# Two weight issues on ScalarE's queue, the first queries between the memory's keys and values, and one more rest on VectorE

## The chip, the cores and the metric

The kernel runs on one core of a Trainium2 chip. The core has TensorE (PE; its weight loads are shown as PEld), VectorE (DVE), ScalarE (ACT), GpSimd (POOL) and SyncE (SP), each with an instruction queue of its own that runs in order, and 16 DMA engines. The metric is device time of one launch, in microseconds, as the median of three runs.

## The reference

One inference step of a one-layer encoder, in float32: 512 prompt tokens and 32 sample tokens with d = 1024.

```
z  = rmsnorm(x, g) @ w_in                     # 3880 columns: qa ka va ga qb kb vb gb qm gm qi ki wi
mk, mv = split(rmsnorm(mem, g_mem) @ w_mem_kv, 2)
oa = band attention(qa, ka, va, bias table)   # 6 heads, own chunk of 64 and 8 before it
ob = attention over the k keys with the highest index score (qi, ki, wi)   # k = 128 prompt, 256 sample
om = attention(qm, mk, mv)                    # 4 heads, 256 memory tokens
x  = x + concat(oa*silu(ga), ob*silu(gb), om*silu(gm)) @ w_out
y  = rmsnorm(x, g_final)
```

The sample's 32 tokens do the same against caches of earlier keys and values. The new keys and values are outputs too.

## The kernel before

Every dense product of the prompt runs as three products of rounded parts: an operand x is split into a high part h (rounded to the format in which TensorE runs fastest) and a rest l = x - h, and x w is h wh + l wh + h wl. In the names, `xTh` and `xTl` are the parts of the scaled, transposed input, `wh` and `wl` those of a weight tile, `mTh` and `mTl` those of the memory. ACT makes the high parts, DVE the rests of x, and a rest of a weight (`tsub`, line 672) is made by GpSimd unless the tile's number stands in `WV` (line 36), in which case by DVE. The first four weight tiles, numbers 0 to 3, are the indexer's (296 columns: 8 index heads, the index key, the head weights), and DVE makes their rests in any case (line 665). Numbers 4 to 7 are ka's, four tiles of 256 rows and 384 columns.

The start (lines 803 to 1085) loads x and the index weights in K tiles of 128 rows, eight of them, two to an `x_load`. For each K tile SP issues a DMA of x (`xr`, 128x544) and one of the weights (`raw`, 128x296); for the first one also the norm's weights `g_mix`. Then SP issues two small tables, ka's weights, the rows of x for the norms, and so on. TensorE begins with matmuls of a tile of ones, which fill its time until the first data is there, and then runs `index_group`: for each K tile three pieces (h wh, h wl, l wh) of three matmuls of 128x296, one for each of the prompt's tiles 1 to 3. More fills with ones go between the pieces. Behind it come packed matmuls of the sample (`raw,xF`), of the first tile's keys (`xr,gw`), and the dense matmuls of ka. The accumulators of the index stage are given back when DVE has rotated them (`rot`, `rt`) and ACT has copied the head weights (`wI`); that of `xr,gw` when ACT has copied it (`k`).

After that the projections follow in the order of `EARLY` and `LATE` (lines 45 and 46), and beside them, as tasks, the indexer's scores, the top-k choice, the three attentions and the sample's share. The sample's index scores are `KSs,QSs`: KSs holds 1024 cached index keys and the new ones, split by ACT and DVE. The sample's threshold is found by a search of sixteen steps in a row, each with two passes on ACT and a one-column matmul (`bf_ok`).

No engine chooses at run time what to do next. When the program is built, a planner (class `Line`) keeps a clock for every engine, with costs for each instruction and rates for transfers (`rate`, line 232). Each task waits until a point of this clock, and so the clock sets the order in which instructions are written into the queues. `warm` (line 916) writes fills with ones where the planner's clock sees TensorE waiting in the index stage. So a changed cost or table can move instructions anywhere behind it, without changing what is computed. Nearly all instructions pass through one helper and have its line, L405; they are told apart by their tiles.

Of the kernel before, what the change touches and what calls it, by code (L numbers as in the profile page):

```python
# [27 lines left out]
QA, KA, VA, GA, QB, KB, VB, GB, QM, GM, QI = 0, 384, 768, 1152, 1536, 1920, 2304, 2688, 3072, 3328, 3584  # L28
# [4 lines left out]
TOPK_S = 256  # L33


WV = (0, 1, 2, 3)
START = "xxxtwwwwrrrrrwmmrr"
SURE = 1.0
SLACK = 1.1
# [2 lines left out]
WARM = 0.1  # L42
LATER = 0.3

EARLY = ("ka", "va", "mk", "mv", "qa0", "qa1", "ga0", "qa2", "ga1", "ga2", "qm0", "gm0", "qm1", "gm1")
LATE = ("gb0", "kb", "qb", "vb", "gb1", "gb2")


class Op:


    def __init__(self, eng, d, share, deps):
        self.eng, self.d, self.share, self.deps = eng, d, share, deps
        self.start = self.end = 0.0
        self.after = {}
# [5 lines left out]
class Free:  # L61


    eng = None
# [24 lines left out]
        return When(self.of, self.by)  # L89


class Line:

    def __init__(self):
        self.clk = {"PE": 1.35, "DVE": 0.7, "ACT": 0.9, "POOL": 1.2, "SP": 0.7}

        self.queue = {e: deque() for e in self.clk}  # L100
        self.base = dict(self.clk, DMA=0.0, array=(0.0, 0.0, 0.0, True))
        self.base.update({"DVE port": 0.0, "POOL port": 0.0})
        self.last = self.base.copy()
        self.writes, self.reads, self.users = {}, {}, {}
        self.boxes = {}
        self.tables = {"exp": (AF.Exp, AF.Tanh)}
        self.table = None
        self.mode, self.short = None, False
        self.tasks = []
        self.seq = 0  # L110
        self.margin = 0.3
        self.time = 0.0
        self.warm = None

    def cost(self, eng, op, outs, ins, kw):
        if eng == "PE":
            n = outs[0].free_size()
# [38 lines left out]
    @staticmethod  # L156
    def lag(of, to):

        if of is None and to == "PE":
            return 0.3  # L160
        if of == to or of is None:
            return 0.127 if to == "DVE" else 0.09 if to == "POOL" else 0.0
        return 0.95 if of == "SP" else 0.26 if to == "PE" else 0.2 if of == "PE" else 0.06 if of == "POOL" else 0.15

    def box(self, x):

# [55 lines left out]
    @staticmethod  # L222
    def shares(op, outs, ins):

        if outs[0].space == PSUM or any(x.space == PSUM for x in ins):
            return False
        full = [x for x in ins if x.free_size() > 1]
        if op in ("scalar_tensor_tensor", "tensor_tensor"):
            return True
        return op in ("tensor_scalar", "tensor_copy") and len(full) > 0 and outs[0].dtype == F32  # L230

    def rate(self):

        t = self.clk["SP"]
        return 340e3 if t < 1 else 170e3 if t < 2.3 else 330e3 if t < 7 else 380e3

    def op(self, eng, op, outs, ins, kw):
        deps = {}
        outs_, ins_ = ([x for x in xs if x.tensor.name in self.writes] for xs in (outs, ins))
        for x in outs_ + ins_:  # L240
            b = self.box(x)
            for w, o in self.writes[x.tensor.name]:
                if all(p[0] < q[1] and q[0] < p[1] for p, q in zip(w, b)):
                    if o.eng is None:
                        for u in o.users.values():
                            deps.setdefault(u, False)
                    else:
                        deps[o] = True
        for x in outs_:
            b = self.box(x)  # L250
            for (w, _), o in self.reads[x.tensor.name].items():
                if all(p[0] < q[1] and q[0] < p[1] for p, q in zip(w, b)):
                    deps.setdefault(o, False)
        d = (outs[0].size() * 4 / self.rate() if eng == "SP" else
             self.cost(eng, op, outs, ins, kw) * (1.0 if eng == "PE" else SLACK))
        share = eng == "POOL" or eng == "DVE" and self.shares(op, outs, ins)
        new = Op(eng, d, share, [(o, w) for o, w in deps.items()])
        for x in outs_:
            n, b = x.tensor.name, self.box(x)
            self.writes[n] = [e for e in self.writes[n]  # L260
                              if not all(q[0] <= p[0] and p[1] <= q[1] for p, q in zip(e[0], b))] + [(b, new)]
            self.reads[n] = {k: o for k, o in self.reads[n].items()
                             if not all(q[0] <= p[0] and p[1] <= q[1] for p, q in zip(k[0], b))}
        for x in ins_:
            self.reads[x.tensor.name][self.box(x), eng] = new
        for x in outs_ + ins_:
            self.users[x.tensor.name][eng] = new

        now = self.now()
        for q in self.queue.values():  # L270
            while q and q[0].start <= now:
                q.popleft().enter(self.base)
        self.queue[eng].append(new)
        if share and self.queue["POOL" if eng == "DVE" else "DVE"]:
            self.last = self.base.copy()
            self.events()
        else:
            self.begin(new, self.start(new))
# [9 lines left out]
    def begin(self, o, t):  # L288
        last = self.last
        o.start = t  # L290
        if o.eng == "SP":
            o.end = max(t + 1.3, last["DMA"]) + o.d
            o.after = {"SP": t + 0.45, "DMA": o.end}
        else:
            d = o.d
            if o.eng == "PE":
                (self.window, self.busy, self.over, self.slow) = last["array"]
                d = self.array(t, d)
            o.end = t + d
            o.after = {o.eng: o.end}  # L300
            if o.eng == "PE":
                o.after["array"] = (self.window, self.busy, self.over, self.slow)
            if o.share:
                o.after[o.eng + " port"] = o.end
        o.enter(last)
        self.clk[o.eng] = o.end if o.eng != "SP" else t

    def events(self):

# [124 lines left out]
def hybrid_step(ctx: ExitStack, tc: tile.TileContext, a: dict):  # L434
    ctx.enter_context(tc.manual_schedule())
    nc = tc.nc
    line = Line()
    V, G, A, PE, DMA = (Timed(line, n, e) for n, e in (("DVE", nc.vector), ("POOL", nc.gpsimd), ("ACT", nc.scalar),
                                                       ("PE", nc.tensor), ("SP", nc.sync)))

    def pool(stack, name, side):
        return Slots(line, stack.enter_context(tc.tile_pool(name=name, bufs=1, side=side, reuse_waits="tile")))
# [65 lines left out]
    ka = va = ysS = None  # L508

    queried, gates = [None] * 3, [None] * 3  # L510
    mk = cp.tile([P, 2, 256], F32, tag="mk", name="mk")
    mv = cp.tile([P, 2, 256], F32, tag="mv", name="mv")
# [25 lines left out]
    def tsub(eng, out, in0, in1):  # L538
        eng.tensor_tensor(out, in0, in1, op=ALU.subtract)

    def f(t):
        return t.bitcast(F32)
# [34 lines left out]
    w_in, w_out, w_mem = a["w_in"], a["w_out"], a["w_mem_kv"]  # L577
    NATURAL = {"i": (QI, 296), "ka": (KA, 384), "va": (VA, 384), "kb": (KB, 384), "qb": (QB, 384), "vb": (VB, 384)}
    TURNED = {"qa": QA, "ga": GA, "qm": QM, "gm": GM, "gb": GB}
    for nm in ("i",) + EARLY + LATE:  # L580
        if nm in NATURAL:
# [49 lines left out]
    def w_split():  # L631
        at = {}
        for i in range(len(w_list)):
# [37 lines left out]
            yield line.at(wh) - 0.2  # L671
            tsub(V if i in WV else G, wl, raw, f(wh))
            split.append((wh, wl))
# [131 lines left out]
    def x_load():  # L805

        c = len(x_raw)
        yield from ()
        t = (rp.tile([P, 2, N], F32, tag="xr", name="xr", bufs=3) if c < 3 else
             cp.tile([P, 2, N], F32, tag="gate1", name="xr"))  # L810
        if c % 2 == 0:
            firsts.append(cp.tile([P, 2, 2, 296], F32, tag=("q0", "gate0")[c // 2], name="raw"))
        raw = firsts[c // 2][:, c % 2]
        for kk in range(2):
            rows = slice((2 * c + kk) * P, (2 * c + kk + 1) * P)
            if c == kk == 0:
                DMA.dma_start(t[:, kk, :], a["x_t"][rows, :])
                DMA.dma_start(gT[0], a["norm_mix_g"])
            DMA.dma_start(raw[:, kk, :], w_in[rows, QI:QI + 296])
            if c + kk > 0:  # L820
                DMA.dma_start(t[:, kk, :], a["x_t"][rows, :])
        raws.append(raw)
        x_raw.append(t)
# [80 lines left out]

    over = {}
    line.until(lambda g=x_load(): next(g, 1) == 1)
    make_identity(nc, ident)
    G.memset(nhalf, -0.5)
# [38 lines left out]
    for nm in ("cos32", "sin32", "cos64", "sin64"):  # L947
        d = int(nm[3:])
# [968 lines left out]
    line.spawn(out_sample())  # L1917
    projections(EARLY)
    projections(LATE)
# [206 lines left out]
```

## Time and profile before

| | us |
|---|---|
| median of three runs | 353.21 (352.42 to 353.29) |
| the profiled execution | 352.53 |
| its span on the core | 350.8 |
| PE busy (2748 matmuls) | 342.6, 98% of the span |
| PEld busy | 300.2, 86% |
| DVE busy | 277.5, 79% |
| ACT busy | 224.2, 64% |
| POOL busy | 174.3, 50% |

The span is what the rows below divide; some 1.7 us of the execution lie around it. Matmuls are pipelined and their ends are modelled, so PE's busy share says that it had work, not that it ran at its peak. The distance between the starts of two matmuls is the better measure of their cost.

### The profile page before, as it was taken

The page shows a single profiled execution, that of the slowest core. Times are in us where ns is not written, and L with a number is a line of the kernel's source. Part 1 is how long each engine was busy: PE and PEld are TensorE (multiplying, and loading weights), DVE is VectorE, ACT ScalarE, POOL GpSimd, SP SyncE. Part 2 cuts the span into 40 slices and gives each one's busy share as a digit, 9 for nine tenths or more (in the row PEclk, how much of TensorE's full clock was granted, in tenths as well). Part 3 has the DMA queues.
Part 4 walks back from the last instruction along what each step waited for, and adds up shares of the span by engine and source line. Part 5 has one row for each costly group of instructions (what it writes and reads, how often), then busy time and mean ns, then how long its engine had stood idle before and what let it go on. Part 6 is the DMA issues. An engine that isn't in the chain of part 4 may idle for free.

```text
span 350.8 us, 7580 instructions
## 1 busy us (share of the span) xinstructions
PE 342.6 (98%) x2748; PEld 300.2 (86%) x2748; DVE 277.5 (79%) x700; ACT 224.2 (64%) x536; POOL 174.3 (50%) x195
## 2 busy tenths in 40 slices
PE   8999999999999999999999999999999999999992
PEld 8979989989999998898898899899986777676882
DVE  3765768699889999997999945798996899674743
ACT  5759678898564876894757427413795786472542
POOL 3468264475554585255634473744471465215622
PEclk9999999999999999999999999999999999999998
DMA  7999542456538251343231232232372537300033
GB/s 230 323 360 354 134 140 75 143 162 152 151 92 296 66 144 39 78 127 88 76 91 45 93 124 58 60 93 98 95 284 92 180 106 265 114 0 2 0 111 143
DMA packets 39604, 46.31 MB, mean 132 GB/s; under 512 B 5360, under 2 KB 32624, under 8 KB 39568
## 3 DMA queue, kind: packets, MB, share of 16 engines
q1 hardware_dynamic: 39568, 45.85, 42.0%
q8 instruction: 21, 0.34, 0.4%
q14 instruction: 15, 0.12, 0.1%
HBM read 39.67 MB, written 6.16 MB: 131 GB/s over the span
## 4 chain that ended last, share of the span: by engine, by line
PE 95%; DVE 1%; ACT 1%; issue 1%; POOLq 0%; POOL 0%; ACTq 0%; DVEq 0%
PE bank L405 95%; DVE rot L405 1%; DVE xr L405 0%; ACT junkS L405 0%; DVE rt L405 0%; ACT wh L405 0%; ACT sq L405 0%; POOLq L2114 0%; POOL xr L405 0%; ACT bf_ok L405 0%; ACT k L405 0%; POOL ss L405 0%; ACT wI L405 0%; DVE ones L405 0%; ACTq L405 0%
## 5 line engine op out<-in xcount | busy, mean ns | idle before, releaser
L405 POOL TENSOR_TENSOR wl<-raw,wh 128x512 fp32r<-128x512 f32 (+1 forms) x69 | 104.5, 1523 | 79.9 <-ACT wh L405 68.2
L405 ACT ACTIVATE wh<-raw 128x512 fp32r<-128x512 f32 (+2 forms) x77 | 50.7, 662 | 23.4 <-PE bank L405 12.0
L405 PE MATMUL bank<-wh,xTh 128*128 128x384 f32 (+1 forms) x184 | 61.2, 347 | 0.2 <-ACT k L405 0.2
L405 PE MATMUL bank<-wl,xTh 128*128 128x384 f32 (+1 forms) x184 | 58.8, 334 | 0.0
L405 PE MATMUL bank<-wh,xTl 128*128 128x384 f32 (+1 forms) x184 | 58.5, 332 | 0.0
L405 ACT ACTIVATE z<-z,st 128x256 f32<-128x256 f32 (+3 forms) x80 | 42.4, 553 | 18.9 <-DVE st L405 18.7
L405 PE MATMUL bank<-xTh,wh 128*128 128x272 f32 x208 | 46.3, 303 | 0.0
L405 PE MATMUL bank<-xTl,wh 128*128 128x272 f32 x208 | 43.0, 288 | 0.0
L405 PE MATMUL bank<-xTh,wl 128*128 128x272 f32 x208 | 42.9, 288 | 0.0
L405 PEld LDWEIGHTS bank<-wh,xTh 128*128 128x128 f32 x184 | 34.1, 190 | 1.8 <-ACT wI L405 0.6
L405 PEld LDWEIGHTS bank<-xTh,wh 128*128 128x128 f32 x208 | 32.7, 189 | 2.7 <-issue 1.8
L405 PEld LDWEIGHTS bank<-wl,xTh 128*128 128x128 f32 x184 | 34.1, 190 | 0.0
L405 PEld LDWEIGHTS bank<-wh,xTl 128*128 128x128 f32 x184 | 33.9, 189 | 0.1
L405 PEld LDWEIGHTS bank<-xTl,wh 128*128 128x128 f32 x208 | 32.6, 188 | 0.0
L405 PEld LDWEIGHTS bank<-xTh,wl 128*128 128x128 f32 x208 | 32.6, 189 | 0.0
L405 DVE MAX8 m<-ysel 128x8 f32<-128x256 f32 (+2 forms) x48 | 26.5, 552 | 0.1
L405 DVE MATCH_REPLACE8 ysel<-m,ysel 128x256 f32<-128x256 f32 (+2 forms) x48 | 26.0, 542 | 0.0
L405 PE MATMUL bank<-ident,z 128*128 128x128 f32 (+1 forms) x162 | 24.8, 274 | 0.0
L405 ACT ACTIVATE junkS<-ysS,bi 128x1056 int8<-128x1056 f32 x16 | 18.8, 1172 | 6.8 <-DVE bi L405 5.7
L405 PEld LDWEIGHTS bank<-ident,z 128*128 128x128 f32 (+1 forms) x162 | 18.6, 140 | 5.1 <-issue 1.6
L405 ACT COPY z<-bank 128x512 f32<-128x512 f32 (+2 forms) x31 | 15.7, 520 | 10.2 <-PE bank L405 8.5
L405 DVE SCALAR_TENSOR_TENSOR ysel<-r,wI,ysel 128x256 f32<-128x256 f32 (+2 forms) x21 | 19.7, 938 | 2.4 <-ACT r L405 1.8
(299 smaller groups left out, 784.1 us busy)
## 6 DMA issues: line engine op xcount, KB each, us to landing
raw<-in_w_in_dram SPq DMA_DIRECT2D x20, 384.0 KB, 3.7
raw<-in_w_in_dram SPq DMA_DIRECT2D x26, 256.0 KB, 2.9
raw<-in_w_out_dram SPq DMA_DIRECT2D x16, 256.0 KB, 3.6
xr<-in_x_t_dram SPq DMA_DIRECT2D x8, 272.0 KB, 4.4
nat<-in_x_prompt_dram SPq DMA_DIRECT2D x4, 512.0 KB, 7.7
raw<-in_w_mem_kv_dram SPq DMA_DIRECT2D x8, 256.0 KB, 2.7
xr<-in_x_prompt_dram SPq DMA_DIRECT2D x4, 512.0 KB, 3.3
out_dram<-xr SPq DMA_DIRECT2D x4, 512.0 KB, 2.6
```

The lines of the kernel that those rows point to most:

```text
L405: return fn(*args, **kw)
```

## The change

Three things are edited by hand. The index weights of the first two K tiles (the first `x_load`) are issued on ACT's queue (`DMA2`), beside SP's. In `EARLY` the first tile of qa comes between the memory's keys mk and its values mv. And `WV` has a fifth number, 7: the rest of ka's fourth weight tile is made by DVE. The planner learns of the second queue ("ACTQ"), and its rate of transfers becomes 250 GB/s for the first microsecond and 380 GB/s behind it. Everything else that moves is moved by the planner's clock.

```
-WV = (0, 1, 2, 3)
+WV = (0, 1, 2, 3, 7)
-EARLY = ("ka", "va", "mk", "mv", "qa0", "qa1", "ga0", "qa2", "ga1", "ga2", "qm0", "gm0", "qm1", "gm1")
+EARLY = ("ka", "va", "mk", "qa0", "mv", "qa1", "ga0", "qa2", "ga1", "ga2", "qm0", "gm0", "qm1", "gm1")
+QUEUES = "SP", "ACTQ"
...
-        self.clk = {"PE": 1.35, "DVE": 0.7, "ACT": 0.9, "POOL": 1.2, "SP": 0.7}
+        self.clk = {"PE": 1.35, "DVE": 0.7, "ACT": 0.9, "POOL": 1.2, "SP": 0.7, "ACTQ": 0.7}
...
-        return 340e3 if t < 1 else 170e3 if t < 2.3 else 330e3 if t < 7 else 380e3
+        return 250e3 if t < 1 else 380e3
...
-        if o.eng == "SP":
+        if o.eng in QUEUES:
             o.end = max(t + 1.3, last["DMA"]) + o.d
-            o.after = {"SP": t + 0.45, "DMA": o.end}
+            o.after = {o.eng: t + 0.45, "DMA": o.end}
...
+    DMA2 = Timed(line, "ACTQ", nc.scalar)
...
-            DMA.dma_start(raw[:, kk, :], w_in[rows, QI:QI + 296])
+            (DMA2 if c == 0 else DMA).dma_start(raw[:, kk, :], w_in[rows, QI:QI + 296])
```

The helper's line is L408 in the changed kernel. Its first rows on TensorE's queue, in the index stage, read so before (`ones` is the fill, xTh and xTl the parts of x, x10 that ten follow one another):

```order
L405 MATMUL bank<-ones 128x128 x10
L405 MATMUL bank<-wh,xTh_81 128x296 x3
L405 MATMUL bank<-wl,xTh_81 128x296 x3
L405 MATMUL bank<-wh,xTl_83 128x296 x3
L405 MATMUL bank<-ones 128x128 x3
L405 MATMUL bank<-wh,xTh_81 128x296 x3
L405 MATMUL bank<-wl,xTh_81 128x296 x3
L405 MATMUL bank<-wh,xTl_83 128x296 x3
L405 MATMUL bank<-wh,xTh_81 128x296 x3
L405 MATMUL bank<-wl,xTh_81 128x296 x3
L405 MATMUL bank<-ones 128x128 x2
L405 MATMUL bank<-wh,xTl_83 128x296 x3
```

and so now:

```order
L408 MATMUL bank<-ones 128x128 x9
L408 MATMUL bank<-wh,xTh_81 128x296 x3
L408 MATMUL bank<-wl,xTh_81 128x296 x3
L408 MATMUL bank<-wh,xTl_83 128x296 x3
L408 MATMUL bank<-wh,xTh_81 128x296 x3
L408 MATMUL bank<-ones 128x128 x3
L408 MATMUL bank<-wl,xTh_81 128x296 x3
L408 MATMUL bank<-wh,xTl_83 128x296 x3
L408 MATMUL bank<-wh,xTh_81 128x296 x3
```

Nine fills stand at the start instead of ten, the three behind the first K tile stand inside the second one, and the two in the third K tile are gone, as are two more ahead of the last piece of the stage. The 72 index matmuls are the same.

On ACT's queue, at the end of the index stage (wh of ka's weight tiles, wI the head weights, k the first tile's keys, zS the sample's row), before:

```order
L405 ACTIVATE xTh_82<-xr,g_mix 128x544
L405 ACTIVATE wh<-raw 128x768 x2
L405 ACTIVATE wI<-bank 128x8 x3
L405 ACTIVATE wh<-raw 128x768
L405 COPY k_365<-bank 128x128
L405 COPY zS<-bank 32x296
```

and now:

```order
L408 ACTIVATE xTh_82<-xr,g_mix 128x544
L408 ACTIVATE wh<-raw 128x296
L408 ACTIVATE wh<-raw 128x768 x3
L408 ACTIVATE wI<-bank 128x8 x3
L408 COPY k_361<-bank 128x128
L408 ACTIVATE junk,ss<-nat 128x1024
L408 COPY zS<-bank 32x296
```

All three wh of ka come ahead of wI now, none stands between wI and k, and the last index weights' wh comes behind the last x.

Further on in ACT's queue, around the sample's index keys KSs (rb the norms spread over tokens, QSs and kst the sample's index queries and key), before:

```order
L405 ACTIVATE wh<-raw 128x768
L405 ACTIVATE ka<-bank,rs 128x384 x4
L405 ACTIVATE junk,ss<-nat 128x1024
L405 ACTIVATE mTh<-mr,g_mem 128x256
L405 ACTIVATE wh<-raw 128x768
L405 ACTIVATE KS<-bank 128x512
L405 ACTIVATE stk<-rot 128x16x32
L405 ACTIVATE QSs<-bank 128x256
L405 ACTIVATE kst_700<-rotS 32x64
L405 ACTIVATE KSs<-cbi 128x1024
```

and now:

```order
L408 COPY rb<-bank 128x32
L408 ACTIVATE mTh<-mr,g_mem 128x256
L408 ACTIVATE wh<-raw 128x768
L408 ACTIVATE ka<-bank,rs 128x384 x2
L408 ACTIVATE QSs<-bank 128x256
L408 ACTIVATE kst_619<-rotS 32x64
L408 ACTIVATE KSs<-cbi 128x1024
L408 ACTIVATE junk,ss<-nat 128x1024
L408 ACTIVATE KS<-bank 128x512
```

The sample's keys are made ahead of the prompt's KS now, and two of ka's four scalings have gone to DVE. TensorE's `KSs,QSs` moves with them: 114 dense matmuls of 128x384 stand ahead of it instead of 144. In all, DVE has five more instructions, GpSimd one fewer, ACT two fewer besides its two DMA issues, and TensorE five fills fewer.

## Rows read from the trace of the kernel before

**Rows 1.** Chain of waits, in order of time: start us, us, what.

```profile
21.92 0.18 ACT wI L405
22.10 0.20 ACT wh L405
...
22.73 0.27 ACT k L405
...
23.04 47.29 PE bank L405 x307
...
137.73 204.03 PE bank L405 x1640
```

**Rows 2.** Table of TensorE's waits: engine, tile, waited for, total us, times, longest.

```profile
PE bank L405 <- ACT bf_ok L405: 0.7, 1, 0.7
```

**Rows 3.** Timeline of ACT: start us, us, instruction, [idle before, what ended it].

```profile
3.86 0.75 ACT L405 ACTIVATE xTh<-xr,g_mix 128x544 fp32r<-128x544 f32 x1 [1.63 <-DMA g_mix<-in_norm_mix_g_dram]
...
6.60 0.75 ACT L405 ACTIVATE xTh<-xr,g_mix 128x544 fp32r<-128x544 f32 x1 [0.22 <-DMA xr<-in_x_t_dram]
...
13.53 0.75 ACT L405 ACTIVATE xTh<-xr,g_mix 128x544 fp32r<-128x544 f32 x1 [0.31 <-DMA xr<-in_x_t_dram]
```

**Rows 4.** Windows: stretch and us, busy per engine, PEclk, DMA share, GB/s.

```profile
3.50:5.00 1.50, 1.50 (x9) 1.50 (x8) 0.36 (x1) 1.09 (x2) 0.00 (x0) 1.00 0.82 211
5.00:8.00 3.00, 3.00 (x20) 3.00 (x18) 1.88 (x4) 1.85 (x4) 0.61 (x2) 1.00 0.97 326
8.00:13.00 5.00, 5.00 (x39) 5.00 (x38) 5.00 (x10) 4.86 (x10) 2.57 (x5) 1.00 1.08 369
...
20.00:36.00 16.00, 15.83 (x95) 14.76 (x88) 9.39 (x24) 12.40 (x26) 11.03 (x19) 1.00 1.06 344
```

**Rows 5.** Timeline of SP's queue: when it issues the first transfers.

```profile
1.17 0.42 SPq L405 DMA_DIRECT2D g_mix<-in_norm_mix_g_dram  x1
1.63 0.90 SPq L405 DMA_DIRECT2D raw<-in_w_in_dram  x2
...
2.57 0.43 SPq L405 DMA_DIRECT2D xr<-in_x_t_dram  x1
```

**Rows 6.** Timeline of TensorE in the index stage.

```profile
6.22 0.88 PE L405 MATMUL bank<-wl,xTh 128*128 128x296 f32 x3
...
6.94 0.57 PE L405 MATMUL bank<-wh,xTl 128*128 128x296 f32 x3
...
7.35 0.83 PE L405 MATMUL bank<-ones 128*128 128x128 f32 x6
...
7.93 0.66 PE L405 MATMUL bank<-wh,xTh 128*128 128x296 f32 x3
...
9.68 0.57 PE L405 MATMUL bank<-wl,xTh 128*128 128x296 f32 x3
...
10.09 0.60 PE L405 MATMUL bank<-ones 128*128 128x128 f32 x4
...
10.94 0.57 PE L405 MATMUL bank<-wh,xTh 128*128 128x296 f32 x3
...
16.65 0.61 PE L405 MATMUL bank<-ones 128*128 128x128 f32 x4
```

**Rows 7.** Timeline of TensorE's weight loads and matmuls at the start of ka.

```profile
19.69 0.18 PEld L405 LDWEIGHTS bank<-raw,xF 128*32 128x32 f32 x6 [0.21 <-issue]
20.50 0.19 PEld L405 LDWEIGHTS bank<-wh,xTh 128*128 128x128 f32 x1 [0.63 <-ACT wI L405]
...
22.54 0.34 PE L405 MATMUL bank<-wl,xTh 128*128 128x384 f32 x1
```

**Rows 8.** Timeline: GpSimd's rest of ka's fourth tile, and the sample's index keys.

```profile
31.75 1.82 POOL L405 TENSOR_TENSOR wl<-raw,wh 128x768 fp32r<-128x768 f32 x1
...
47.95 1.22 DVE L405 TENSOR_TENSOR KSs<-cbi,KSs 64x1024 fp32r<-64x1024 f32 x1 [0.28 <-ACT KSs L405]
...
51.26 0.63 PE L405 MATMUL bank<-KSs,QSs 128*128 128x512 f32 x2
```

More of the change, by code (lines that the diff above doesn't have):

```diff
@@ L162, in lag @@
             return 0.127 if to == "DVE" else 0.09 if to == "POOL" else 0.0
-        return 0.95 if of == "SP" else 0.26 if to == "PE" else 0.2 if of == "PE" else 0.06 if of == "POOL" else 0.15
+        return 0.95 if of in QUEUES else 0.26 if to == "PE" else 0.2 if of == "PE" else 0.06 if of == "POOL" else 0.15
     def box(self, x):
@@ L253, in op @@
                     deps.setdefault(o, False)
-        d = (outs[0].size() * 4 / self.rate() if eng == "SP" else
+        d = (outs[0].size() * 4 / self.rate() if eng in QUEUES else
              self.cost(eng, op, outs, ins, kw) * (1.0 if eng == "PE" else SLACK))
@@ L305, in begin @@
         o.enter(last)
-        self.clk[o.eng] = o.end if o.eng != "SP" else t
+        self.clk[o.eng] = o.end if o.eng not in QUEUES else t
     def events(self):
```

## The prediction, as put on record before the result

> **What bounds the kernel now.** I read the chain of waits first. From 23.04 us it is TensorE work to 341.78 us, broken only near 71 us, and its last piece is 204.03 us long [rows 1]. So after about 23 us the end is set by how much TensorE has to do, and what is left to win lies in the start, in the rare waits of TensorE, and in the tail of some 6.5 us, which the change does not touch (TensorE's last 45 rows are the same in both orders). The table of waits agrees: in the body TensorE waits 0.7 us once for ACT's bf_ok, a step of the search for the sample's threshold [rows 2].
>
> The start is two things running side by side. One is data. ACT makes the high parts of x, and its rows say what it waited for: first for g_mix until 3.86 us, then for x's second tile until 6.60, and for the last until 13.53 [rows 3]. Six tiles between 6.60 and 13.53 make 1.16 us per K tile (x and its weights, 430 KB). The windows show the DMA engines at 211 GB/s with a share of 0.82 between 3.5 and 5 us, 326 GB/s at 0.97 up to 8 us, and 369 GB/s at 1.08 from 8 to 13 us [rows 4]: the stretch 3.5 to 5 is the poor one. The issue rows show why it can be poor: SP issues g_mix at 1.17, two weight tiles from 1.63, and x's second tile only at 2.57 [rows 5]. g_mix is 4 KB and a weight tile 148 KB, so over 1.4 us the queue is given 300 KB, about 220 GB/s.
>
> The other is TensorE itself. Its 72 index matmuls come in pieces of three. A piece takes 0.72 us at 6.22 and 0.41 us at 9.68 [rows 6]: the lower of the two clock levels (1.2 GHz) before about 7 us, the higher (2.4 GHz) after. From 7.93 us it never waits again in this stretch, while ACT's last x is done at 14.28 and TensorE is still at its index matmuls after 16.65 [rows 3, 6]. So it, not the data, ends the index stage. Two fills with `ones` stand in that run, at 10.09 and at 16.65. From 10.09 to 10.94 a fill and one piece take 0.85 us, a piece alone 0.41: a fill costs 0.44 us [rows 6].
>
> Behind it data counts again: the sample's ka matmuls wait for the last of ka's four weight tiles until 19.69, and the dense ka matmuls start at 20.50, their weight load having waited for ACT's wI [rows 7]. The third group of accumulators is held until 23.04: DVE's rotations, ACT's wI at 21.92, ACT's wh (128x768) at 22.10, ACT's k at 22.73, then TensorE [rows 1].
>
> **The change part by part.**
>
> *Fewer fills.* TensorE's order has `ones` x10, x3, x2, x2 before and x9, x3 after. The x10 runs before any data is there. The x3 stands before: from 7.35 to 7.93, 0.58 us, where x's second tile was just coming (ACT done at 6.60 + 0.75 = 7.35) [rows 3, 6]. After, it stands inside the second K tile: the same cost in another place. The two x2 go: 2 x 0.44 = 0.88 us off a run that TensorE bounds.
>
> *Two weight issues on ACT's queue.* SP's issues are 0.47 us apart, so everything from x's second tile on is issued 0.94 us earlier [rows 5]. Call s what arrives earlier of that. Its bounds are 0 (the engines were the limit) and 0.94. If the stretch from 3.5 to 5 us ran at the 326 GB/s of the next one, (326 - 211) x 1.5 = 173 KB would be ahead, 0.47 us at 369 GB/s; at 369 itself, 0.64 [rows 4]. Keeping the pair's issue distance, it is 0.94. I take 0.8. The issue on ACT is not in this trace; by SP's rows it is 0.4 to 0.5 us each, and it delays the table load and one small ACT instruction that are hidden, since ACT idles 1.63 us before 3.86 [rows 3]. Beyond 1.63 us for both it would delay x's first tile.
>
> The Trainium skill speaks against this part (DMA: Bandwidth & Descriptors, "Issuing engines are not separate DMA queues"): transfers started by different engines run on the same 16 DMA engines, and starting them from several saves only the time that the sequencer needs to issue. The trace agrees that this time is short, and by that rule s would be 0 wherever the engines are full, as at the share of 1.08; it makes the first rival below.
>
> *What it costs the first tile.* x's first tile and g_mix now share the engines with weights that came later before. If half of a tile's 148 KB goes ahead of them at 211 GB/s, that is 0.36 us; the bounds are 0 and the whole tile, 0.72 us [rows 4]. Call it d; I take 0.1, near the lower end: the engines' share was below 1 in the stretch just behind [rows 4], so there was room beside x's first tile, and that tile is issued as early as before. Nothing excludes a loss; a gain is excluded, as no issue ahead of x's first tile goes.
>
> *Start, summed.* TensorE ends its index stage 0.88 - d = 0.78 us earlier. ka's fourth weight tile comes s = 0.8 earlier, at 18.9. Both must hold, the smaller counts: 0.78, and the dense ka matmuls start near 19.7.
>
> *ACT's order behind the index stage.* Before: wh x2, wI x3, wh, k. After: wh x3, wI x3, k. The wh no longer stands between wI and k; in the chain it is most of the 0.63 us from 22.10 to 22.73 [rows 1]. wI comes after the third rotation, at 21.92 - 0.78 = 21.1, and k is done 0.3 later at 21.4, when TensorE wants the bank only at 21.9: the twelfth dense matmul came 2.04 us after the first before, at 22.54, and a thirteenth would have followed 0.17 us later [rows 7]. The wait is gone: 23.04 less 22.71, 0.33 us. The new order has its own wait: the third wh stands ahead of wI and needs ka's third weight tile, and behind it wait the three wI and k, and with them TensorE's banks. That tile comes before the fourth (18.9); if it came only with it, wh would end near 19.6 and the dense matmuls would start about 0.4 later than 19.7. Bounds: 0.33 gained, 0.4 lost by that or by GpSimd's three wl, now without a pause, slowing DVE's rotations; I take the gain, since the tiles come one behind the other.
>
> *wl of the fourth ka tile on DVE.* GpSimd loses 1.82 us [rows 8]. DVE gains one TENSOR_TENSOR of 128x768; its KSs of 64x1024 took 1.22 us [rows 8], so 0.9 by the share of elements, 1.22 at most. It lands in 25 to 30 us, where TensorE waits for neither. Cost 0; GpSimd's wl ended at 33.57, and TensorE, a microsecond earlier now, would come closer to it, so without this edit a few tenths could be lost.
>
> *qa0 between mk and mv.* The same matmuls; SP issues two qa tiles between mk's and mv's weights. mv is read first in the attention, far behind. Cost 0.
>
> *The search.* Sixteen bf_ok steps, one waited 0.7 us [rows 2]. All sixteen stand elsewhere now, and SP's, DVE's and ACT's orders in the body are shuffled. I take half of it away, 0.35; bounds 0.7 gained and 1.4 lost (two new waits of its kind).
>
> Sum: 0.78 + 0.33 + 0.35 = 1.46 us. The profiled execution took 352.53 us (span 350.8), so 351.07. The median of the runs is 353.21, 0.68 above it; on that scale 351.75, and I say **351.7 us**. The likeliest case's own range is 350.9 to 352.4.
>
> **The rivals.**
>
> *The DMA engines were the limit (s = 0).* For it: share 0.97 from 5 us on. Against it: 211 GB/s at a share of 0.82 between 3.5 and 5. Then ka's weights come at 19.69 as before, the dense matmuls start 0.05 us earlier at most, and only 0.33 and 0.35 are left: 353.21 - 0.7 = 352.5.
>
> *The clock rises later.* After, nine instead of ten `ones` precede the first piece, and that piece comes d later, so TensorE idles 0.4 to 1 us before it, where it was busy without a gap before. If the lower level then lasts for two more K tiles, each costs 9 matmuls at 0.24 instead of 0.137, 0.93 us [rows 6]: 351.7 + 1.9 = 353.6. The Trainium skill (TensorE: Matmul & The Clock Gate, "Part 1: The HAM clock gate") calls the lower level the default and activity what releases it; the rows show only that it rose once TensorE had been busy from the start.
>
> *TensorE runs into the sample's index keys (slower).* KSs,QSs stands behind 114 dense matmuls of 128x384 instead of 144: 30 x 0.175 = 5.3 us earlier, and with the start 1.1 more, at 44.9 instead of 51.26 [rows 8]. KSs was finished on DVE at 49.17 [rows 8]. ACT has KSs earlier in its queue too, behind two ka instead of four and no 128x512 KS, and ACT had room before (12.40 of 16 us from 20 to 36 [rows 4]). But if the chain through ACT and DVE comes earlier only by the start's 1.1 us, it ends at 48.1 and TensorE, in order, waits 48.1 - 44.9 = 3.2 us, with everything behind it: 351.7 + 3.2 = 354.9. It decides from the point where KSs ends after 44.9; about 2.5 us after that the kernel is slower.
>
> **Chances.** 0.3% (about 1.06 us) is what a measurement of this kernel tells from no change: faster is below 352.15, slower above 354.27. Forecast 0.50 (0.45 of it below 352.15). DMA engines 0.18 (0.04 faster, 0.14 same). Clock 0.13 (0.10 same, 0.02 slower, 0.01 faster). Index keys 0.12 (0.11 slower). More than forecast, with all waits gone and s at 0.94, near 350.5: 0.07. Faster 0.57, same 0.30, slower 0.13. The range 350.2 to 353.8 holds the forecast, the DMA and most of the clock case, and the gain's upper end: about 0.83.
>
> **What would show it.** Right: the first piece of TensorE with xTh near 5.4 and ACT waiting for x's second tile until 5.7 to 5.9 instead of 6.60; the index stage over near 16.7; the dense ka matmuls from 19.7; no wait of TensorE for ACT's k; a PE table of waits with at most one bf_ok. Wrong: pieces of 0.72 us after 7.5 us (clock); ka's fourth weight tile still landing at 19.7 (DMA); a wait of TensorE before KSs,QSs, identR,stk or r,wsel between 36 and 60 us (index keys).

## The result and the profile after

| kernel | runs | median us | lowest to highest |
|---|---|---|---|
| before | 8 | 352.96 | 352.41 to 353.85 |
| changed | 8 | 354.94 | 353.52 to 356.27 |

The ratio of the two is 1.0054, with a 95% interval of 1.0036 to 1.0071: the change makes the kernel slower by 1.9 us (1.3 to 2.5). The forecast was 351.7, with a range up to 353.8. The profiled execution took 355.0 us, with a span of 353.2. Against the profile before, the span is 2.4 us longer. What follows says where these 2.4 us lie.

In this profile the start went as forecast or better. ACT's timeline, beside its own queue (`ACTq`) with the two weight issues [rows 3]:

```profile
0.73 0.89 ACTq L408 DMA_DIRECT2D raw<-in_w_in_dram  x2
...
4.36 0.75 ACT L408 ACTIVATE xTh<-xr,g_mix 128x544 fp32r<-128x544 f32 x1 [1.22 <-DMA g_mix<-in_norm_mix_g_dram]
...
5.36 0.74 ACT L408 ACTIVATE xTh<-xr,g_mix 128x544 fp32r<-128x544 f32 x1
...
12.61 0.75 ACT L408 ACTIVATE xTh<-xr,g_mix 128x544 fp32r<-128x544 f32 x1 [0.22 <-DMA xr<-in_x_t_dram]
```

x's first tile is taken up at 4.36 instead of 3.86, the second at 5.36, without a wait, instead of 6.60, and the last at 12.61 instead of 13.53. That is not one execution's luck: in the eight profiles of this case in which ACT's queue has the two issues, the second tile is taken up between 5.33 and 5.82, and in the five in which SP's has them between 6.13 and 6.60. The windows [rows 4] show where that comes from: from 3.5 to 8 us the DMA engines move 368 and 384 GB/s, where they moved 211 and 326.

```profile
3.50:5.00 1.50, 1.50 (x9) 1.41 (x7) 0.00 (x0) 0.64 (x1) 0.29 (x1) 1.00 1.07 368
5.00:8.00 3.00, 2.33 (x15) 1.98 (x15) 2.65 (x5) 2.53 (x7) 1.10 (x3) 1.00 1.03 384
```

TensorE's timeline [rows 6, 7]: the first piece at 5.50, two short waits, pieces of 0.41 us from 6.98 on, the last index piece at 16.26, and the dense ka matmuls from 19.61 instead of 20.50.

```profile
5.50 0.68 PE L408 MATMUL bank<-wh,xTh 128*128 128x296 f32 x3 [0.40 <-ACT wh L408]
6.46 0.68 PE L408 MATMUL bank<-wl,xTh 128*128 128x296 f32 x3 [0.27 <-DVE wl L408]
6.98 0.57 PE L408 MATMUL bank<-wh,xTl 128*128 128x296 f32 x3
...
16.26 0.57 PE L408 MATMUL bank<-wh,xTl 128*128 128x296 f32 x3
...
19.61 0.44 PE L408 MATMUL bank<-wh,xTh 128*128 128x384 f32 x1
```

So this profile is 0.89 us ahead by 20 us into the span. TensorE's waits [rows 2] and the chain [rows 1] show where that was lost. In the table (engine, tile, waited for, total us, times, longest) the bf_ok wait is gone, and a wait for the sample's B keys has come, the longest one behind the start:

```profile
PE bank L408 <- DMA keysB<-in_cache_b_k_dram: 1.7, 1, 1.7
...
PE bank L408 <- DVE ysS L408: 0.3, 1, 0.3
PE bank L408 <- ACT z L408: 0.3, 1, 0.3
```

The chain (start us, us, what) no longer runs through TensorE alone. From 41.02 to 52.08 it runs through ACT and DVE, up to the ysS of the waits. At 258 us it leaves TensorE again, for SP's queue and a transfer of 6.82 us:

```profile
6.46 34.56 PE bank L408 x254
...
41.04 0.60 ACT KS L408
...
52.08 206.13 PE bank L408 x1692
...
258.23 0.33 SPq L408
...
259.08 6.82 DMA keysB<-in_cache_b_k_dram
...
265.94 1.12 PE bank L408 x12
```

`keysB` are the cached keys of the sample's B attention, three tiles of 512 KB. SP issues them behind three tiles of x_prompt (`xr`), which take the place of x's parts. TensorE's last reads of x hold the third of those back (SP's longest wait for TensorE is 4.0 us here and was 3.5 before). Behind it the keys stand in SP's queue. The waits of SP's queue between 243 and 262 us, in the changed kernel and before (waited for, total us, times, longest):

```profile
SPq L408 <- PE bank L408: 6.8, 2, 4.0
```
```profile
SPq L405 <- PE bank L405: 6.7, 2, 3.5
```

SP's and TensorE's timelines of the changed kernel, and the times from issue to landing of its three key tiles:

```profile
253.29 5.27 SPq L408 DMA_DIRECT2D xr<-in_x_prompt_dram  x3
258.60 1.38 SPq L408 DMA_DIRECT2D keysB<-in_cache_b_k_dram  x3
```
```profile
263.19 1.05 PE L408 MATMUL bank<-keysB,qbS 64*32 64x512 f32 x4 [0.29 <-ACT z L408]
265.94 1.97 PE L408 MATMUL bank<-keysB,qbS 64*32 64x512 f32 x20 [1.71 <-DMA keysB<-in_cache_b_k_dram]
267.84 1.97 PE L408 MATMUL bank<-z,mv 128*64 128x128 f32 x32
```
```profile
DMA to landing us min/median/max: 4.5/6.8/7.6
```

and the same places in the kernel before:

```profile
253.99 4.41 SPq L405 DMA_DIRECT2D xr<-in_x_prompt_dram  x3
258.45 1.38 SPq L405 DMA_DIRECT2D keysB<-in_cache_b_k_dram  x3
```
```profile
267.70 1.98 PE L405 MATMUL bank<-keysB,qbS 64*32 64x512 f32 x24
269.61 0.55 PE L405 MATMUL bank<-ident,z 128*128 128x128 f32 x3
```
```profile
DMA to landing us min/median/max: 4.3/5.8/6.7
```

The issue time hardly moved (258.60 against 258.45). What moved is the order on TensorE: before, `oM` and `oA` products and 32 `z,mv` stand ahead of the 24 score matmuls, which then take 1.91 us (267.70 to 269.61). Now the scores come first, at 263.19, and take 4.65 us (263.19 to 267.84). The difference is 2.74 us. What the scores wait for is the second key tile, issued at 259.08 and landed 6.82 us later, at 265.90. The first four score matmuls need only the first tile and run at 263.19, but they save nothing: the other twenty take 1.90 us from 265.94, as long as all 24 did before. So the wait costs the whole stretch from 263.19 to 265.94, and not only the 1.71 us that the table counts, from the end of the four. Before, the second tile was issued at 258.92 and landed 5.8 us later, and the scores found it there.

Just ahead of this place TensorE was some 0.7 us earlier than before (the first `wh,oAh` at 260.21 against 260.93, with the same matmuls done), and 0.7 - 2.7 leaves 2.0 of the 2.4 us; the other 0.4 are not traced here. These 0.7 are not the start's 0.89 carried through, though the numbers are close. In the profile of e3 (below), which has the same order of TensorE up to there, the dense ka matmuls begin 1.0 us later, at 20.62, and yet the `KSs,QSs` that waits for ysS here (52.08) runs at 52.15 and the first `wh,oAh` at 260.19.

### The profile page after: what moved, and what is told of

Read it like the earlier page. It is cut to its first block, busy times and chain, and to the rows that moved or that the text cites. A ratio compares the mean times of both kernels' runs of the same rounds, so it can differ in the third digit from the quotient of the medians.

```text
span 353.2 us, 7563 instructions
## 1 busy us (share of the span) xinstructions
PE 343.0 (97%) x2738; PEld 298.7 (85%) x2738; DVE 277.3 (78%) x705; ACT 224.1 (63%) x532; POOL 176.4 (50%) x194
## 4 chain that ended last, share of the span: by engine, by line
PE 90%; DMA 3%; DVE 2%; issue 2%; ACT 1%; SPq 0%; POOLq 0%; POOL 0%; DVEq 0%; ACTq 0%
PE bank L408 90%; DMA keysB<-in_cache_b_k_dram 2%; DMA g_mix<-in_norm_mix_g_dram 1%; DVE ysel L408 1%; DVE xr L408 0%; SPq L408 0%; DVE mTl L408 0%; DVE stk L408 0%; ACT xTh L408 0%; ACT sq L408 0%; ACT wh L408 0%; ACT KS L408 0%; POOLq L2119 0%; DVE vaS L408 0%; DVE wl L408 0%
## 5 line engine op out<-in xcount | busy, mean ns | idle before, releaser
L408 POOL TENSOR_TENSOR wl<-raw,wh 128x512 fp32r<-128x512 f32 (+1 forms) x68 | 102.5, 1519 | 75.5 <-ACT wh L408 69.2
L408 ACT ACTIVATE wh<-raw 128x512 fp32r<-128x512 f32 (+2 forms) x77 | 50.4, 663 | 23.3 <-PE bank L408 11.2
L408 PE MATMUL bank<-wh,xTh 128*128 128x384 f32 (+1 forms) x184 | 60.6, 343 | 0.4 <-ACT wh L408 0.4
L408 PE MATMUL bank<-wl,xTh 128*128 128x384 f32 (+1 forms) x184 | 58.7, 333 | 0.3 <-DVE wl L408 0.3
L408 PE MATMUL bank<-wh,xTl 128*128 128x384 f32 (+1 forms) x184 | 58.4, 332 | 0.0
L408 ACT ACTIVATE z<-z,st 128x256 f32<-128x256 f32 (+3 forms) x78 | 41.6, 553 | 21.1 <-DVE st L408 21.0
L408 PE MATMUL bank<-xTh,wh 128*128 128x272 f32 x208 | 46.3, 303 | 0.0
L408 PE MATMUL bank<-xTh,wl 128*128 128x272 f32 x208 | 43.0, 288 | 0.0
L408 PE MATMUL bank<-xTl,wh 128*128 128x272 f32 x208 | 43.0, 288 | 0.0
L408 PEld LDWEIGHTS bank<-wh,xTh 128*128 128x128 f32 x184 | 33.8, 188 | 1.9 <-ACT wI L408 0.6
L408 PEld LDWEIGHTS bank<-wl,xTh 128*128 128x128 f32 x184 | 33.7, 188 | 0.5 <-DVE wl L408 0.5
L408 PEld LDWEIGHTS bank<-wh,xTl 128*128 128x128 f32 x184 | 33.9, 189 | 0.0
L408 PEld LDWEIGHTS bank<-xTh,wh 128*128 128x128 f32 x208 | 32.5, 189 | 1.3 <-issue 0.9
L408 PEld LDWEIGHTS bank<-xTl,wh 128*128 128x128 f32 x208 | 32.6, 188 | 0.0
L408 PEld LDWEIGHTS bank<-xTh,wl 128*128 128x128 f32 x208 | 32.6, 189 | 0.0
L408 DVE MAX8 m<-ysel 128x8 f32<-128x256 f32 (+2 forms) x48 | 26.5, 552 | 0.2
L408 DVE MATCH_REPLACE8 ysel<-m,ysel 128x256 f32<-128x256 f32 (+2 forms) x48 | 26.1, 543 | 0.0
L408 PE MATMUL bank<-ident,z 128*128 128x128 f32 (+1 forms) x162 | 25.0, 274 | 0.0
L408 DVE SCALAR_TENSOR_TENSOR ysel<-r,wI,ysel 128x256 f32<-128x256 f32 (+2 forms) x21 | 19.2, 914 | 6.1 <-ACT r L408 5.5
L408 PEld LDWEIGHTS bank<-ident,z 128*128 128x128 f32 (+1 forms) x162 | 18.5, 140 | 5.0 <-issue 2.0
L408 ACT COPY z<-bank 128x384 f32<-128x384 f32 (+2 forms) x33 | 16.7, 513 | 8.3 <-PE bank L408 7.7
L408 ACT ACTIVATE junkS<-ysS,bi 128x1056 int8<-128x1056 f32 x16 | 18.8, 1173 | 3.8 <-DVE bi L408 2.7
```

Of the source, the lines that this page charges most:

```text
L408: return fn(*args, **kw)
```

## The experiments

Theory A: the start gained what was forecast, and the loss is TensorE's wait for the sample's B keys, in an order that asks for them before they can be there. Theory B: issuing weights on ACT's queue costs the kernel. Rival C: the loss is spread over the new interleaving of sample and dense matmuls. All ratios are to the kernel before, on the same chip; e1 to e4, e5 to e8 and e9 to e11 are three sessions, each on another chip.

| kernel | median us | ratio, 95% interval |
|---|---|---|
| e1_queue_alone | 353.12 | 0.9997 (0.9985 to 1.0009) |
| e2_order_alone | 355.63 | 1.0062 (1.0037 to 1.0087) |
| e3_keys_before_x | 351.93 | 0.9975 (0.9957 to 0.9994) |
| e4_scores_later | 351.48 | 0.9952 (0.9937 to 0.9968) |
| e5_fills_back | 352.66 | 1.0002 (0.9989 to 1.0014) |
| e6_both_remedies | 351.75 | 0.9964 (0.9950 to 0.9978) |
| e7_early_undone | 355.78 | 1.0084 (1.0064 to 1.0104) |
| e8_rest_undone | 355.85 | 1.0106 (1.0062 to 1.0149) |
| e9_before_keys_first | 353.43 | 1.0005 (0.9992 to 1.0019) |
| e10_later_sp | 351.81 | 0.9973 (0.9960 to 0.9986) |
| e11_later_sp_fills | 353.18 | 1.0010 (0.9997 to 1.0023) |

### The queue and the order, each by itself

e1, the kernel before with the planner told nothing:

```
+    DMA2 = Timed(line, "SP", nc.scalar)
...
+            (DMA2 if c == 0 else DMA).dma_start(raw[:, kk, :], w_in[rows, QI:QI + 296])
```

> The order of every engine as before; only the first two index weights are issued on ScalarE's queue. Theory A (the queue move is harmless and worth something only where TensorE does not bound the start; the loss of the changed kernel comes from its new order): TensorE still runs all four fills, so its index stage ends within 0.4 us of before and the time is 352.96 +- 0.5 us, no difference that can be measured, although x's second tile lands near 5.2 instead of 6.58. Theory B (issuing on ScalarE costs the kernel, by the delay of x's first tile or of ScalarE's own start): 354 to 355 us, as the changed kernel.

Measured: 353.12 us, the same as before. Theory B falls.

e2, the changed kernel with its order, the two weights back on SP:

```
-    DMA2 = Timed(line, "ACTQ", nc.scalar)
+    DMA2 = Timed(line, "ACTQ", nc.sync)
```

> The order of every engine as after; only the two weights go back to SyncE's queue. Theory A: the start loses what the queue gave, x's second tile lands near 6.6 and ka's fourth weight tile near 19.7, the dense ka matmuls start near 20.4, and the rest of the changed kernel stays as it is, its wait for the sample's B keys included: 354.94 + 0.9 = 355.8 us. Theory B (the queue costs): the loss goes with the queue, 352.5 to 353.3 us.

Measured: 355.63 us. The order alone makes the loss. TensorE waits in the start for ka's weights, and still for the keys:

```profile
20.26 1.80 PE L408 MATMUL bank<-raw,xF 128*32 128x384 f32 x8 [0.86 <-DMA raw<-in_w_in_dram]
...
267.24 1.97 PE L408 MATMUL bank<-keysB,qbS 64*32 64x512 f32 x20 [0.68 <-DMA keysB<-in_cache_b_k_dram]
```

### The keys' wait taken away, in two ways

e3, the changed kernel; SP issues the keys ahead of the third x tile:

```
-    for t in range(NT - 1):
+    for t in range(2):
         DMA.dma_start(xr[t], a["x_prompt"][t * P:(t + 1) * P, :])
...
         for m, t in enumerate(kt):
             DMA.dma_start(t[:, 0:PAST], a["cache_b_k"][m * P:(m + 1) * P, :])
+        for t in range(2, NT - 1):
+            DMA.dma_start(xr[t], a["x_prompt"][t * P:(t + 1) * P, :])
```

> The order of TensorE, VectorE, ScalarE and GpSimd as after; SyncE issues the three transfers of the sample's B keys ahead of the third x_prompt tile (which waits for TensorE until 258.2 us) instead of behind it. Theory A (the wait of TensorE for those keys, 1.71 + 0.29 us and an unlisted 0.7 beside it, is the loss): keys issued near 254.2 land by 260, no wait of TensorE for them, 354.94 - 2.7 = 352.2 us. Rival C (the loss is spread over the new interleaving of sample and dense matmuls, and the keys' wait hides other waits): 354.3 us or more.

e4, the changed kernel; the scores are held 3 us longer in the planner's clock, so that other work goes ahead:

```
-        yield line.sure(qT, *kt)
+        yield line.sure(qT, *kt) + (3.0 if mix == 1 else 0.0)
```

> As after, but the planner holds the sample's B scores 3 us longer behind their keys, so that w_out matmuls stand ahead of them as in the kernel before; orders up to 263 us are those of after. Theory A: no wait for the keys, 354.94 - 2.7 = 352.2 us, the same as with the keys issued earlier, within 0.6. Rival C: 354.3 us or more, with other waits behind 268 us.

Measured: 351.93 and 351.48 us, 3.0 and 3.5 us below the changed kernel, and both faster than the kernel before, with intervals that leave 1 out. SP's and TensorE's timelines of e3:

```profile
253.27 0.81 SPq L408 DMA_DIRECT2D xr<-in_x_prompt_dram  x2
254.12 4.89 SPq L408 DMA_DIRECT2D keysB<-in_cache_b_k_dram  x3
259.06 0.43 SPq L408 DMA_DIRECT2D xr<-in_x_prompt_dram  x1
```
```profile
262.81 1.98 PE L408 MATMUL bank<-keysB,qbS 64*32 64x512 f32 x24
264.72 1.97 PE L408 MATMUL bank<-z,mv 128*64 128x128 f32 x32
```

One detail of the expectation was off: only the first key tile goes early. The other two lie in the same freed space and were held back as well (4.89 us for three issues). The three landed 3.7 to 5.0 us behind their issue, where they had taken 4.5 to 7.6. One tile early, and one x tile fewer ahead of the others, is enough: with the order as in the changed kernel, the 24 scores take 1.91 us again. In e4 they stand at 273.31 and take 1.98. Theory A stands, by two edits that have little in common but the wait they remove. Rival C falls as the main cause.

e6, both edits together:

> Scores held later and the keys' transfers ahead of the third x tile, together. Theory A (the only thing that either remedy removes is the one wait): no gain beyond the better of the two, 351.5 +- 0.5 us. Rival C' (the transfers' burst near 260 us also costs elsewhere): 350.9 us or less.

Measured: 351.75 us, no more than either alone. e9, e3's edit in the kernel before:

> The kernel before with the three transfers of the sample's B keys ahead of the third x tile, all other orders as before. Theory A (what the same edit gave the changed kernel was the removed wait, not a better use of the DMA engines): before, the keys landed at 266.08 and were wanted at 267.70, so there is nothing to gain: 352.9 +- 0.4 us. Rival C' (the transfers' burst costs by itself): 352.2 us or less.

Measured: 353.43 us, no gain (0.1 above the range of theory A). The edit is worth something only where the keys are late.

### The start's two terms, without the keys' wait

e5 puts four fills into e4 (two pairs, ahead of the last piece of the third and the eighth K tile), unknown to the planner, so that nothing else moves:

```
+        if real[0] in (24, 69):
+            for _ in range(2):
+                nc.tensor.matmul(idle[:, 0:P], ones, ones, start=True, stop=True)
+        real[0] += 1
```

> The kernel with the scores held later, plus the four fills of before (two pairs, in the third and the eighth K tile of the index stage), put in without the planner's knowledge, so that nothing else moves. If TensorE bounds the index stage, as the prediction's first term has it (2 x 0.44 us): dense ka matmuls 0.9 us later and 351.48 + 0.9 = 352.4 us. If the data of ka bounds it: 351.5 us, as without them.

e10 is e4 with the weights on SP's queue, and e11 is e10 with e5's fills:

> The kernel with the scores held later, with the first two weights on SyncE's queue: the queue's term of the prediction by itself, without the keys' wait. By the prediction (the smaller of both terms counts, and without the queue the data of ka bounds): x's second tile near 6.6, a wait of TensorE for ka's weights, dense ka 0.8 us later or more, 351.48 + 0.8 = 352.3 us. If the queue was worth nothing: 351.5 us.

> As the one before, and the four fills put back too: neither term of the start. If the smaller of the two terms counts, the fills now stand in time in which TensorE waits for data: no later than the one before by more than 0.4 us, 352.3 to 352.7 us. If the terms add: 352.3 + 0.9 = 353.2 us.

Measured medians, all in e4's order:

| | weights on ACT's queue | on SP's queue |
|---|---|---|
| no extra fills | 351.48 (e4) | 351.81 (e10) |
| four fills | 352.66 (e5) | 353.18 (e11) |

The fills are worth 1.2 and 1.4 us, the queue 0.3 and 0.5. By the ratios they are 1.8 and 1.3 and 0.7 and 0.3 (0.0050, 0.0037, 0.0021 and 0.0008 of 353). The fills' effect is outside the intervals. The queue's is not: the intervals of e4 and e10 overlap, and so do those of e5 and e11. Within this noise the terms add up, and the fills gain as much without the queue as with it. The profiles show less than was expected of them: in e5's the dense ka matmuls begin at 20.50, 0.66 us behind e4's 19.84, and e10's has no wait of TensorE for ka's weights.

One execution of e10, the profiled one, was its longest (353.11 us, where its median is 351.81), and it shows what the rival of the late clock meant. TensorE waited 0.61 us before its first piece at 5.86, and pieces of 0.74 us, those of the lower level [rows 6], lasted to 9.86, with three fills in 0.87 us instead of 0.58:

```profile
8.25 0.94 PE L408 MATMUL bank<-wh,xTh 128*128 128x296 f32 x3
8.99 1.11 PE L408 MATMUL bank<-ones 128*128 128x128 f32 x6
9.86 0.66 PE L408 MATMUL bank<-wl,xTh 128*128 128x296 f32 x3
```
```profile
8.00:10.00 2.00, 2.00 (x12) 2.00 (x12) 1.97 (x5) 1.79 (x4) 0.90 (x2) 1.00 1.04 381
```

The window's granted clock reads 1.00 there all the same; the duration of the pieces is the better sign. The changed kernel did not have this: TensorE waited 0.40 us before its first piece too, but that piece is busy for 0.68 us, where e10's is for 1.11 and that of the kernel before for 1.09. What decides when the level rises in an execution, no run here shows.

### The other two edits undone

e7 is the changed kernel with `"mk", "mv", "qa0"` again, and e8 with `WV = (0, 1, 2, 3)` again. Each gets another order from the planner.

> The changed kernel with mv ahead of qa0 again: start and queue as after, another order behind it. In the planner's own clock the scores then stand 8.6 us behind the landing of their keys (2.3 in the changed kernel, 8.3 before). Theory A: no wait of TensorE for the keys, 352.0 +- 0.8 us. Rival C (the start's gain is lost anyway in the body): 353.5 us or more, without a wait for the keys.

> The changed kernel with ka's fourth low part on GpSimd again. The planner's clock has 2.3 us between the keys and their scores, as in the changed kernel, but also a pause of 3.4 us near 39 us, in which TensorE waits for GpSimd's wl. If the chip has that pause: the keys are waited for as in the changed kernel, and 355 us or more. If the chip does not have it, TensorE runs some 3 us ahead of its plan, the keys are later still against it, and the wait is longer: 355 us or more again. Rival E (running ahead moves SyncE's transfers just as far, since they wait for TensorE): 352 to 353.5 us.

Measured: 355.78 and 355.85 us. For e7 theory A's number was wrong by 3.8 us, and by the words of the expectation rival C came out: the time is over 353.5, without a wait for the keys. The order has another wait, of TensorE for DVE:

```profile
287.16 0.66 PE L408 MATMUL bank<-ident,kb 128*128 128x128 f32 x4 [1.23 <-DVE st L408]
```

That explains 1.2 of the 4.3 us to e4. No run here separates the rest. So an order of this planner can lose as much without the keys; that the changed kernel's own loss is the keys' wait rests on e3 and e4. e8 came out by the first of its branches: TensorE waits twice for GpSimd's wl, 3.3 us in all, and again for the keys. (The profiled execution took 359.52 us, the longest of e8 and 3.7 us above its median.)

```profile
43.41 0.45 PE L408 MATMUL bank<-wl,xTh 128*128 128x384 f32 x1 [2.12 <-POOL wl L408]
...
270.47 1.97 PE L408 MATMUL bank<-keysB,qbS 64*32 64x512 f32 x20 [1.58 <-DMA keysB<-in_cache_b_k_dram]
```

Of these two edits, only undoing the one in `EARLY` (e7) brings the scores back behind their keys, and undoing either gives no faster kernel. The planner's new transfer rates were not undone by any run.

## Why the prediction was wrong

**The step that failed** is the one that priced the rest of the order, and beneath it the path: "So after about 23 us the end is set by how much TensorE has to do". For the search it says "SP's, DVE's and ACT's orders in the body are shuffled. I take half of it away, 0.35; bounds 0.7 gained and 1.4 lost", and for qa0 "Cost 0". The new order cost 2.7 us at one place in the profile, where the chain leaves TensorE for a transfer, and 3.0 to 3.5 by e3 and e4, twice the bound. I had bounded an unknown wait by the one wait that TensorE had before. A better bound was in the trace: the keys were issued only from 258.45 on, held by TensorE's own reads of x, and the second of them landed at 264.7 and was wanted at 267.70. An order that asks for it 4.5 us earlier, at 263.2, had to wait some 1.5 us, and it did not have to be run to see that. The other 1.2 us come from the transfer, which took 6.8 us instead of 5.8 and was issued 0.16 later; why it took longer is not shown, and in e2, with the same order, it took 5.7. I compared TensorE's last 45 rows and the start, not the place between.

Why the planner wrote that order can be read in its own clock, which the kernel's code works out (no time of the chip). It knows of no wait of the third x tile for x's last readers. It lets that tile go at 252.0 and has the last key tile landed at 260.9, 2.3 ahead of the scores at 263.2. On the chip that tile is issued at 258.23, and the second key tile lands at 265.90. In the order before, the clock had 8.3 us between the two, and this slack hid the same blind spot. The clock and the chip agree on the scores themselves (263.2 and 263.19). The fault is the missing wait, not a drift.

**Fills.** The sign and the place were right. The kernels' times give more than 0.88: 1.2 to 1.8 by e5 against e4, and 1.3 to 1.4 by e11 against e10. In e5's profile a pair of fills and the piece behind it take 0.86 us (10.14 to 11.00) and a piece alone 0.41, so a pair costs the 0.44 of the forecast there; where the rest lies is not shown.

**The queue's s and d.** s was taken as 0.8, and in the profile x's second tile is taken up 1.24 us earlier and the last 0.92. d was taken as 0.1 and is 0.5 (4.36 against 3.86). What both are worth to the kernel is 0.3 to 0.7 us by e4, e5, e10 and e11, and 0.1 in e1, never clear of the noise. That "the smaller counts" is not what e10 and e11 show: fills taken away help with the old queue as much. As it stands in the table above, the start gave 1.7 us together (351.48 against 353.18) where the forecast had 0.78.

The Trainium skill's rule (DMA: Bandwidth & Descriptors, "Issuing engines are not separate DMA queues") has only the sequencer's issue time to be saved. The issues came 0.94 earlier and the data 0.92 to 1.24 earlier, so the trace agrees with it in size, and not with the rival that I drew from it (s = 0): between 3.5 and 5 us the engines were not full (211 GB/s before, 368 in the changed kernel), and there the issue time came back as earlier data.

**The k wait, 0.33.** It is not gone for good. The profiles of the changed kernel, e2, e3 and e6 have none, but e4's, e5's, e10's and e11's, whose order is the same there, have 0.3 to 0.7 (here e4's):

```profile
PE bank L408 <- ACT k L408: 0.7, 1, 0.7
PE bank L408 <- DVE ysS L408: 0.5, 1, 0.5
```

The likely cause stood among the prediction's bounds, though no run tests it alone: "GpSimd's three wl, now without a pause, slowing DVE's rotations". The first rotation's last instruction takes 1.39 to 2.00 us in the four with the wait, beside GpSimd's wl, and 0.54 in the changed kernel; the later rotations, wI and k follow behind it. The changed kernel's and e4's:

```profile
17.45 0.54 DVE L408 TENSOR_TENSOR rot<-rt,rot 128x288 f32<-128x288 f32 x1
```
```profile
17.68 1.83 DVE L408 TENSOR_TENSOR rot<-rt,rot 128x288 f32<-128x288 f32 x1
```

It is not the whole condition: in e6 it takes 2.14, the dense ka matmuls begin late (20.74), and there is no wait for k.

**bf_ok, 0.35.** The 0.7 us are gone in the changed kernel, and a wait for ysS of 0.3 to 0.5 has come (not in e3). Net of everything in the new order but the fills, the queue and the keys, e11 stands 0.35 us above before (-0.1 to 0.8), where 0.68 of gain had been counted for k and bf_ok.

**The rival of the index keys** gave 354.9, the number measured, by a mechanism that did not happen. KSs came earlier by itself, at 40.67 on DVE, and TensorE's first product with it ran at 45.25 without a wait:

```profile
45.25 0.63 PE L408 MATMUL bank<-KSs,QSs 128*128 128x512 f32 x2
...
52.08 0.74 PE L408 MATMUL bank<-KSs,QSs 128*128 128x512 f32 x2 [0.32 <-DVE ysS L408]
```

Its frame was right (the order asks for something earlier than its chain can give it), its object was not, and that the number agrees is luck.

**The rest on DVE.** Forecast 0.9, measured 0.93 us (128x768 at 29.03), hidden. Without it, in e8's order, TensorE waits 1.2 us at 35.86 for GpSimd's rest of that tile and 2.1 at 43.41 for a later one, not "a few tenths".

**The account**, from the kernel before: order +0.35 (e11), fills and queue -1.7 (e11 to e4), keys +3.5 (e4 to the changed kernel): 355.1, against 354.94 measured. It is a chain of differences between sessions, so that it closes says only that they agree.

## What to carry to other kernels

Where a planner writes the order, a small gain at the start moves every later demand, so look for the transfers whose issue is tied to the very engine that gets faster: they do not come earlier with it. For each place where the order asks for a transfer earlier than before, read in the old trace when its issue was released and when it landed, and count what is missing as a wait. It is a lower bound (here 1.5 of 2.7 us), since the transfer itself can take longer. Then either issue it ahead of the blocked one or let other work go first: here both turned 1.9 us of loss into a gain, 351.48 us against 352.96 at best.

## What the runs showed of the hardware that was not expected

The same instruction took four times as long on DVE beside GpSimd. Two `mTl` of 128x256 follow one another in the changed kernel, 0.47 us and 2.05 us long, and the second runs beside two `wl` of GpSimd. The next `ysel` takes 2.05 as well, and 0.46 once GpSimd is done:

```profile
45.90 0.47 DVE L408 SCALAR_TENSOR_TENSOR mTl<-mr,g_mem,mTh 128x256 fp32r<-128x256 f32 x1
...
46.56 2.05 DVE L408 SCALAR_TENSOR_TENSOR mTl<-mr,g_mem,mTh 128x256 fp32r<-128x256 f32 x1
48.54 2.05 DVE L408 SCALAR_TENSOR_TENSOR ysel<-r,wI,ysel 128x256 f32<-128x256 f32 x1
...
51.10 0.46 DVE L408 SCALAR_TENSOR_TENSOR ysel<-r,wI,ysel 128x256 f32<-128x256 f32 x1
```
```profile
46.35 3.96 POOL L408 TENSOR_TENSOR wl<-raw,wh 128x768 fp32r<-128x768 f32 x2
```

Each of the two lasts about as long as the GpSimd instruction beside it (3.96 us for two), and they stand ahead of the ysS (DVE, 51.59) that TensorE waits for at 52.08. The Trainium skill (SBUF — State Buffer, "SBUF: two separate sides") calls the pair of ports that both engines share an exclusive lock, held for a whole instruction; these rows agree.

The start is not the same in every execution, though nothing in it changed. e9 has the order and the queues of the kernel before up to 250 us, yet waits 0.38 us for ka's weights and begins the dense matmuls at 21.81 instead of 20.50 (the eight packed matmuls behind the wait take most of the rest):

```profile
20.06 1.82 PE L405 MATMUL bank<-raw,xF 128*32 128x384 f32 x8 [0.38 <-DMA raw<-in_w_in_dram]
21.81 0.45 PE L405 MATMUL bank<-wh,xTh 128*128 128x384 f32 x1
```

Its span is 351.8, against 350.8. In e3 and the changed kernel, with the same start, they begin at 20.62 and 19.61. So a single profile of this start is good to no better than 1 us; for less than that the medians decide.
